# Hybrid encoder layer on one core: norm loads moved to ACT's queue, two additions and one product moved between engines, loads and gates reordered

## The chip, the cores and the metric

One core of a Trainium2 chip runs the whole layer. The metric is the device time of one launch in microseconds (us). Engines are called as in the profile: PE (matrix products), PEld (its weight loads), DVE, ACT and POOL (GpSimd), and SP, which here only issues transfers (DMAs). ACT and POOL issue DMAs too. Each engine works through its own list of instructions in order.

## What is computed

The input is 2048 positions of 1024 channels. One layer has three branches that share one input projection of the normalised input:

```
h = rms_norm(x, norm_g);  z = h @ w_in
ya = fourier_mix(za) * silu(za_gate)                       # branch A
yb = rwkv7_bidir(centred_shift(z_rwkv)) * silu(zb_gate)    # branch B
yc = mla(zq, zkv, zkr) * silu(zc_gate)                     # branch C, attention of 6 heads
merged = sum of sigmoid(z_merge[n]) * (y_n @ proj_n)
out = rms_norm(x + merged @ w_out, final_g)
```

Branch B is a recurrence with a 64x64 state for each of 6 heads, once forward and once backward in time; the two outputs y[0] + y[1] are summed and normalised head by head (mean, variance), and a bonus is added:

```
bonus = einsum('bthn,btdhn,hn->bth', r, k_dir, r_k);   y + bonus[..., None] * v
```

## The kernel before, in words

In order of time (the stretches are those of the profiled execution):

- Up to about 515 us: norm of x, first columns of the input projection, preparation of the attention.
- 515 to 930 us: `columns()` goes on with the projection on PE (L142 to L144 are the three products of one block). Between its blocks PE does the pieces of `units()`, the preparation of branch B: 24 windows (3 channel groups p of 128 channels x 8 stretches u of 256 positions), each for 2 directions d, so 48 sets. One set is: `unit_lora` loads the low-rank input `ul`; `unit_lowrank` (PE) makes `wps`; `unit_decay` turns it into `th`, `ia` (ACT, L656 to L659), the running sum `ls` (DVE, L662 for d=0, L664 for d=1), `ge` (ACT), `kd` or `kds`, and `BK` (half on DVE, half on POOL, L691 and L692); `unit_x` makes `X` (DVE and POOL, L701 and L702); `unit_gram` makes the small products and masks them (DVE, L718 and L720), and SP stores X.
- In the second set of a window, `unit_values` copies the transposed v to `vt` (ACT, L631) and SP stores it. One set later `unit_bonus` multiplies the bonus sum `bp` (PE, L731) by v into `bv` (L733), and SP stores `bv` (L734). `vt` and `bv` have the same tag "vt", with one buffer: `vt` of a window can be written only when `bv` of the window before has landed in memory. In ACT's list `vt` stands ahead of `th` of its set.
- 930 to 1475 us: the rest of the projection (merge gates z, then the attention's gates `gc`), the Fourier branch, and `inverses` (a chain of DVE operations, L758 and L760). Its last results are stored, and `recurrence` loads them: `seq_load` (L969 loads X, L971 loads W), first products `sps` (L984).
- 1475 to 1938 us: attention on PE (`scores`, `softmax`, `probs`, `values`) with the recurrence's 32 steps between its pieces. A unit is 128 queries of one head: four blocks `sc` of scores (L142 to L144), their eviction to S (DVE, L1307), exp (ACT, L1314), four transposes `tp` (PE, L1322) copied to `PT` (L1032 on DVE or L1033 on ACT, `ptd` says which).
- 1938 to 2262 us: attention with `rwkv_out` between its pieces: 8 blocks of 256 positions, each with loads (L1050: `ry0`, `ry1`, `rbv`, `rg`), the sum y + y1 (L1062), mean, variance, and the store. Then first weights of the output stage. From the end of the recurrence on, `self.merged` is true.
- 2262 to 2632 us: output stage.

What sets the order: the pieces of PE are placed by hand, and the background work is a generator (units, then inverses, then recurrence, then rwkv_out) that the columns or the attention advance by `step()`, two steps to an attention unit. A `yield` more or fewer in the generator so moves its PE work by a quarter of a unit. `wait2` is the number of empty steps ahead of the recurrence. The other engines' lists are made by a scheduler from what is emitted; the tile pools add the waits for free buffers.

Of the kernel before, what the change touches and what calls it, by code (L numbers as in the profile page):

```python
# [9 lines left out]
F32 = mybir.dt.float32  # L10
F32R = mybir.dt.float32r
I32 = mybir.dt.int32
AF = mybir.ActivationFunctionType
# [4 lines left out]
P = 128  # L18
# [72 lines left out]
class Trunk:  # L91
    def __init__(self, tc, ins, out, stop=99):
# [39 lines left out]
        self.wait2 = 12  # L132
# [226 lines left out]
    def columns(self):  # L359
# [8 lines left out]
        gates = [(O_ZCG + n * P, self.to_gate(self.gc_d[n], self.nc.gpsimd)) for n in range(3)]  # L368
        self.inproj(gates[0][0], P, gates[0][1])
        cols = [(self.weights(c0, P), consume) for c0, consume in gates[1:]]  # L370
        for tb in range(NTB):
            for w, consume in cols:
                self.project(w, P, tb, consume, True)
# [166 lines left out]
    def units(self):  # L540
        tc, nc = self.tc, self.nc
        with tc.tile_pool(name="un", bufs=1, side="right", reuse_waits="tile") as up, \
# [10 lines left out]
            ul = self.unit_lora(opened[0], 0, up)  # L553
# [4 lines left out]
            for s in range(2 * len(wins) + 2):  # L558
# [5 lines left out]
                if s < 2 * len(wins):  # L564
# [5 lines left out]
                    wps = self.unit_lowrank(w, d, ul, gps)  # L570
                    item = self.unit_decay(w, d, wps, up, ge)
# [3 lines left out]
                if s < 2 * len(wins):  # L575
# [4 lines left out]
                    if s + 1 < 2 * len(wins):  # L580
                        ul = self.unit_lora(opened[n + d], 1 - d, up)
# [56 lines left out]
    def unit_lora(self, w, d, up):  # L638
        lo = up.tile([P, 2, UN], F32R, tag="ul", name=f'ul{w["p"]}{w["u"]}{d}', bufs=self.ulb)
        self.nc.sync.dma_start(lo.bitcast(F32), self.lo_d[:, d, :, w["sl"]].rearrange("n p t -> p n t"))  # L640
        return lo
# [9 lines left out]
    def unit_decay(self, w, d, wps, up, ge):  # L651
# [27 lines left out]
        if d == 1:  # L679
            kds = w["kds"]  # L680
            nc.gpsimd.tensor_tensor(kds, kd, kds, ALU.add)
# [46 lines left out]
    def unit_bonus(self, w, up, gps):  # L728
# [4 lines left out]
        nc.vector.tensor_tensor(bv, bp[:, :UN], w["v"], ALU.mult)  # L733
# [200 lines left out]
    def recurrence(self):  # L934
        tc, nc = self.tc, self.nc
        with tc.tile_pool(name="sq", bufs=1, side="right", reuse_waits="tile") as sp, \
# [10 lines left out]
            yield  # L947
# [15 lines left out]
    def seq_load(self, sp, n):  # L963
# [3 lines left out]
        for d in range(2):  # L967
            c = n if d == 0 else NCH - 1 - n
            nc.sync.dma_start(X[:, d].rearrange("p n s t -> p n (s t)"), self.X_d[d][c])  # L969
            for h in range(2):  # L970
                nc.sync.dma_start(W[64 - 64 * h:P - 64 * h, d, :, 2 * h:2 * h + 2, :].rearrange("p n q k -> p n (q k)"),  # L971
                                  self.V_d[c * C:(c + 1) * C, :, h, :])
        return X, W
# [66 lines left out]
    def rwkv_out(self):  # L1040
        tc, nc = self.tc, self.nc
        W = 256
        with tc.tile_pool(name="ro", bufs=3, side="right", reuse_waits="tile") as rp, \
                tc.tile_pool(name="rops", bufs=1, space=PSUM, side="right", reuse_waits="tile") as rps:
            def load(b):
                sl = slice(b * W, (b + 1) * W)
                ts = []
                for n, src in (("ry0", self.y_d[0]), ("ry1", self.y_d[1]), ("rbv", self.bv_d), ("rg", self.gb_d)):
                    t = rp.tile([P, NP, W], F32, tag=n, name=f"{n}{b}")
                    nc.sync.dma_start(t, src[:, :, sl].rearrange("n p t -> p n t"))  # L1050
# [3 lines left out]
            nxt = load(0)  # L1054
            yield
            yield
            for b in range(T // W):
                sl = slice(b * W, (b + 1) * W)
                y, y1, bv, g = nxt
                if b + 1 < T // W:  # L1060
                    nxt = load(b + 1)
                nc.vector.tensor_tensor(y, y, y1, ALU.add)  # L1062
# [3 lines left out]
                yield  # L1066
                mu = rps.tile([P, 4, W], F32, tag="mu", name=f"mu{b}")
# [11 lines left out]
                self.blocksums(var, hi, lo)  # L1079
                va = rp.tile([P, NP, W], F32, tag="rva", name=f"rva{b}", bufs=1)  # L1080
# [235 lines left out]
    def probs(self, u, g):  # L1316
# [7 lines left out]
        self.copy(g in self.ptd, dst, tp)  # L1324

    def values(self, w):
# [4 lines left out]
        def piece(j):  # L1331
            for k in range(2 * j, 2 * j + 2):
# [3 lines left out]

# [160 lines left out]
```

## Time and profile before

| | |
|---|---|
| median of 3 runs | 2632.33 us (2628.31 to 2634.77) |
| profiled execution, its own time | 2634.32 us |
| its span | 2632.5 us |
| PE busy | 2504.7 us, 95% |
| DVE busy | 1737.4 us, 66% |
| ACT busy | 991.9 us, 38% |
| POOL busy | 848.0 us, 32% |
| mean granted clock of PE | 0.982 |

The busy shares are means over stages that differ, so the stages are read apart: which engine waits in each, and for whom. PE is the engine with the most work, and what the other engines cost shows as PE's idle time. The profiled execution is 2.0 us above the median.

### The profile page before, as it was taken

What the parts mean: (1) busy time and instruction counts of PE and PEld (TensorE: products, weight loads), DVE (VectorE), ACT (ScalarE), POOL (GpSimd) and SP (SyncE); (2) the same over time, 40 slices, a digit from 0 to 9 for tenths busy, and PEclk for the clock granted to TensorE, in tenths of its full rate; (3) what the DMA queues carried; (4) which work ended last, traced back from release to release, by engine and by line L of the source; (5) the groups of instructions that cost most, each with busy time, mean ns of one, the idle gap of its engine ahead of it and who ended that gap; (6) DMA issues with size and microseconds to landing.
All of it is one profiled execution on the core that took longest, in us unless ns stands there. A gap on an engine that the chain in (4) does not pass through costs nothing.

```text
span 2632.5 us, 46308 instructions
## 1 busy us (share of the span) xinstructions
PE 2504.7 (95%) x17295; PEld 2040.8 (78%) x17295; DVE 1737.4 (66%) x3432; ACT 991.9 (38%) x1929; POOL 848.0 (32%) x1124
## 2 busy tenths in 40 slices
PE   7989999999999999989998899999998899999998
PEld 6778887877777777768776688878876677799997
DVE  6236564388888859579398567766767787544444
ACT  6354443355555521111113333333355565322221
POOL 2244433355555511212220233323322220334342
PEclk9999999999999999999998899999999999999999
DMA  4353434477777774552733655665544311645452
GB/s 167 95 146 121 149 125 157 141 262 256 245 262 247 246 156 128 130 145 86 136 84 111 157 169 186 192 186 166 174 149 125 101 53 59 194 128 154 131 154 78
DMA packets 318443, 404.86 MB, mean 154 GB/s; under 512 B 56078, under 2 KB 225097, under 8 KB 317130
## 3 DMA queue, kind: packets, MB, share of 16 engines
q1 hardware_dynamic: 310762, 382.99, 49.0%
q0 software_dynamic: 7456, 18.91, 3.0%
q8 instruction: 137, 2.24, 0.4%
q14 instruction: 88, 0.72, 0.1%
HBM read 236.91 MB, written 164.89 MB: 153 GB/s over the span
## 4 chain that ended last, share of the span: by engine, by line
PE 38%; DVE 13%; DMA 8%; issue 4%; POOL 1%; ACT 1%; SPq 1%; DVEq 0%; POOLq 0%; ACTq 0%
PE av L1334 5%; PE tp L1322 4%; DVE M L760 4%; DVE tmp L758 4%; PE sc L142 3%; PE sc L144 2%; PE sc L143 2%; PE po L144 2%; PE po L143 2%; PE po L142 2%; PE p L144 2%; PE p L143 2%; PE p L142 2%; DVE S L1307 1%; PE mm L142 1%
## 5 line engine op out<-in xcount | busy, mean ns | idle before, releaser
L142 PE MATMUL mm<-hh,wh 128*128 128x512 f32 x1536 | 613.8, 400 | 6.5 <-ACT z L483 3.2
L144 PE MATMUL mm<-hh,wl 128*128 128x512 f32 x1536 | 604.0, 394 | 2.8 <-POOL wl L419 2.6
L143 PE MATMUL mm<-hl,wh 128*128 128x512 f32 x1536 | 605.2, 394 | 0.0
L142 PEld LDWEIGHTS mm<-hh,wh 128*128 128x128 f32 x1536 | 291.7, 190 | 72.1 <-ACT z L483 5.2
L144 PEld LDWEIGHTS mm<-hh,wl 128*128 128x128 f32 x1536 | 291.6, 190 | 65.1 <-POOL wl L419 4.1
L143 PEld LDWEIGHTS mm<-hl,wh 128*128 128x128 f32 x1536 | 291.9, 190 | 58.2 <-issue 1.0
L1307 DVE TENSOR_SCALAR_CACHE_REDUCE S<-sc 128x512 f32<-128x512 f32 x384 | 260.7, 688 | 73.2 <-PE sc L144 67.5
L419 POOL TENSOR_TENSOR wl<-wr,wh 128x256 fp32r<-128x256 f32 x192 | 172.2, 910 | 419.1 <-ACT wh L418 406.2
L1322 PEld LDWEIGHTS tp<-c_id,S 128*128 128x128 f32 x1536 | 192.9, 143 | 84.9 <-ACT PT L1033 14.5
L1322 PE MATMUL tp<-c_id,S 128*128 128x128 f32 x1536 | 237.8, 278 | 21.0 <-ACT S L1314 8.6
L1314 ACT ACTIVATE S<-S,m 128x2048 f32<-128x2048 f32 x96 | 192.2, 2003 | 161.7 <-DVE m L1312 161.7
L758 DVE TENSOR_TENSOR tmp<-M 128x62 f32<-128x62 f32 (+30 forms) x186 | 171.7, 923 | 96.5 <-DMA zm_d<-z 41.3
L142 PE MATMUL sc<-K,Q 96*128 96x512 f32 x384 | 188.4, 491 | 19.7 <-DVE S L1307 13.8
L1033 ACT ACTIVATE PT<-tp 128x512 f32<-128x512 f32 x192 | 113.2, 591 | 225.8 <-PE tp L1322 222.7
L1334 PE MATMUL av<-PT,V 128*64 128x256 f32 x1536 | 180.0, 385 | 0.0
L760 DVE TENSOR_TENSOR M<-M,tmp 128x62 f32<-128x62 f32 (+30 forms) x186 | 170.7, 918 | 5.8
L418 ACT ACTIVATE wh<-wr 128x256 fp32r<-128x256 f32 x192 | 74.4, 412 | 238.7 <-DMA wr<-in_w_in_dram 149.2
L144 PE MATMUL sc<-K,Q 96*128 96x512 f32 x384 | 155.4, 405 | 0.0
L143 PE MATMUL sc<-K,Q 96*128 96x512 f32 x384 | 154.8, 403 | 0.0
L483 ACT ACTIVATE z<-mm 128x512 f32<-128x512 f32 (+1 forms) x120 | 70.3, 589 | 217.7 <-PE mm L144 107.2
L1334 PEld LDWEIGHTS av<-PT,V 128*64 128x64 f32 x1536 | 105.4, 137 | 57.8 <-issue 11.2
L1432 POOL TENSOR_TENSOR g<-g 128x256 f32<-128x256 f32 x128 | 98.8, 774 | 143.2 <-DVE g L1430 100.6
(388 smaller groups left out, 4945.4 us busy)
## 6 DMA issues: line engine op xcount, KB each, us to landing
X_d<-X SPq DMA_DIRECT2D x96, 512.0 KB
sX<-X_d SPq DMA_DIRECT2D x64, 768.0 KB
wr<-in_w_in_dram SPq DMA_DIRECT2D x193, 128.0 KB
zm_d<-z SPq DMA_DIRECT2D x96, 256.0 KB
g<-zm_d SPq DMA_DIRECT2D x64, 384.0 KB
uu<-u_d SPq DMA_DIRECT2D x24, 512.0 KB
ul<-lo_d SPq DMA_DIRECT2D x48, 256.0 KB
sW<-V_d SPq DMA_DIRECT2D x128, 96.0 KB
```

The source lines that it names most:

```text
L142: mm(out, lh, rh, start=start, stop=False)
L143: mm(out, lh, rl, start=False, stop=False)
L144: mm(out, ll, rh, start=False, stop=stop)
L419: nc.gpsimd.tensor_tensor(wl[:, ks, :], wr, wh[:, ks, :].bitcast(F32), ALU.subtract)
L758: nc.vector.tensor_tensor(tv, M[:, 0:j, j:j + 1].to_broadcast([P, j, n]), M[:, j:j + 1, j + 1:C].to_broadcast([P, j, n]), ALU.mult)
L760: nc.vector.tensor_tensor(M[:, 0:j, j + 1:C], M[:, 0:j, j + 1:C], tv, ALU.add)
L1033: return self.nc.scalar.activation(out, src, AF.Copy)
L1307: nc.vector.tensor_scalar(u["S"][:, ks], sc, 1.0, -3.4e38, ALU.mult, ALU.max, accum_out=u["m4"][:, kb:kb + 1])
L1314: nc.scalar.activation(S, S, AF.Exp, scale=SM_SCALE, bias=m4[:, 5:6], accum_out=u["win"]["rs"][:, col:col + 1])
L1322: nc.tensor.transpose(tp[:, k, :], u["S"][:, (4 * g + k) * P:(4 * g + k + 1) * P], self.ident)
L1334: nc.tensor.matmul(av[64 * h:64 * h + 64, 0:QB], self.V[:, k, (2 * hp + h) * 64:(2 * hp + h + 1) * 64], PT[k // 4][:, k % 4, h, :], start= ...
L1432: nc.gpsimd.tensor_tensor(g, g, acc, ALU.add)
```

## The change

1. `wait2` goes from 12 to 9, and `recurrence` yields three times instead of once after its first loads: the first loads are emitted three steps earlier and the first products one step earlier, 9 + 3 steps instead of 12 + 1.
2. The gates `gc` are stored from ACT's queue instead of POOL's, and the last two gate columns are done in pairs of position blocks.
3. `unit_lora`'s load `ul` goes from SP's queue to ACT's, half a set earlier (48 loads).
4. The addition of `kds` for d=1 goes from POOL to DVE (24 times).
5. `unit_bonus`: one DVE product becomes a copy by ACT and a product on POOL (24 times).
6. `seq_load` loads W ahead of X.
7. `rwkv_out`: the four loads of a block go from SP's queue to ACT's, two blocks ahead instead of one; the sum y + y1 goes from DVE to POOL, one block ahead; a block has one step more.
8. `probs`: from `merged` on, one of the two copies on DVE goes to ACT.
9. `values`: doubling and inverting the row sums moves from ahead of the first piece into the fourth.

```diff
-        self.wait2 = 12
+        self.wait2 = 9
...
-        gates = [(O_ZCG + n * P, self.to_gate(self.gc_d[n], self.nc.gpsimd)) for n in range(3)]
+        gates = [(O_ZCG + n * P, self.to_gate(self.gc_d[n], self.nc.scalar)) for n in range(3)]
...
-        for tb in range(NTB):
+        for tbs in ((0, 1), (2, 3)):
             for w, consume in cols:
-                self.project(w, P, tb, consume, True)
+                for tb in tbs:
+                    self.project(w, P, tb, consume, True)
...
                     wps = self.unit_lowrank(w, d, ul, gps)
+                    if s + 1 < 2 * len(wins):
+                        ul = self.unit_lora(wins[n + d], 1 - d, up)
...
-                    if s + 1 < 2 * len(wins):
-                        ul = self.unit_lora(opened[n + d], 1 - d, up)
...
-        self.nc.sync.dma_start(lo.bitcast(F32), self.lo_d[:, d, :, w["sl"]].rearrange("n p t -> p n t"))
+        self.nc.scalar.dma_start(lo.bitcast(F32), self.lo_d[:, d, :, u * UN:(u + 1) * UN].rearrange("n p t -> p n t"))
...
-            nc.gpsimd.tensor_tensor(kds, kd, kds, ALU.add)
+            nc.vector.tensor_tensor(kds, kd, kds, ALU.add)
...
-        nc.vector.tensor_tensor(bv, bp[:, :UN], w["v"], ALU.mult)
+        nc.scalar.activation(bv, bp[:, :UN], AF.Copy)
+        nc.gpsimd.tensor_tensor(bv, bv, w["v"], ALU.mult)
...
-            yield
+            for _ in range(3):
+                yield
...
         for d in range(2):
             c = n if d == 0 else NCH - 1 - n
-            nc.sync.dma_start(X[:, d].rearrange("p n s t -> p n (s t)"), self.X_d[d][c])
             for h in range(2):
                 nc.sync.dma_start(W[64 - 64 * h:P - 64 * h, d, :, 2 * h:2 * h + 2, :].rearrange("p n q k -> p n (q k)"),
                                   self.V_d[c * C:(c + 1) * C, :, h, :])
+        for d in range(2):
+            c = n if d == 0 else NCH - 1 - n
+            nc.sync.dma_start(X[:, d].rearrange("p n s t -> p n (s t)"), self.X_d[d][c])
...
-                    nc.sync.dma_start(t, src[:, :, sl].rearrange("n p t -> p n t"))
+                    nc.scalar.dma_start(t, src[:, :, sl].rearrange("n p t -> p n t"))
...
-            nxt = load(0)
+            tiles = [load(0), load(1)]
...
-                nc.vector.tensor_tensor(y, y, y1, ALU.add)
+                if b == 0:
+                    nc.gpsimd.tensor_tensor(y, y, y1, ALU.add)
...
+                yield
+                if b + 2 < T // W:
+                    tiles.append(load(b + 2))
...
+                if b + 1 < T // W:
+                    nc.gpsimd.tensor_tensor(tiles[b + 1][0], tiles[b + 1][0], tiles[b + 1][1], ALU.add)
...
-        self.copy(g in self.ptd, dst, tp)
+        self.copy(g in (self.ptd[1:] if self.merged else self.ptd), dst, tp)
...
+            if j == 3:
+                nc.vector.tensor_scalar(rs, rs, 2.0, None, ALU.mult)
+                nc.vector.reciprocal(rs, rs)
...
-        nc.vector.tensor_scalar(rs, rs, 2.0, None, ALU.mult)
-        nc.vector.reciprocal(rs, rs)
```

How instructions move, at three places. In the names, the figures after the letters are p, u and d, so `bv12` is the bonus of p=1, u=2, and `BK130` is of p=1, u=3, d=0; the last number only tells tiles apart. The lines of the changed kernel are some lower or higher numbers than those of before for the same code (L692 is there L694).

POOL in the units, p=1, window u=3, direction d=0, before:

```order
404 L673 COPY gc_127<-ge0_4620 128x4
405 L701 TENSOR_TENSOR X130_6929<-uu13_6709,ge0_4620 64x4x64
406 L702 TENSOR_TENSOR X130_6929<-uu13_6709,ge0_4620 64x4x64
407 L691 TENSOR_TENSOR BK130_6865<-ia130_6852,th130_6850 64x4x64
408 L692 TENSOR_TENSOR BK130_6865<-kds13_6860,th130_6850 64x4x64
409 L419 TENSOR_TENSOR wl3488_7344<-wr3488_0_7345,wh3488_7343 128x256
```

and now, the same place:

```order
403 L675 COPY gc_127<-ge0_4620 128x4
404 L703 TENSOR_TENSOR X130_6940<-uu13_6721,ge0_4620 64x4x64
405 L704 TENSOR_TENSOR X130_6940<-uu13_6721,ge0_4620 64x4x64
406 L693 TENSOR_TENSOR BK130_6877<-ia130_6864,th130_6862 64x4x64
407 L694 TENSOR_TENSOR BK130_6877<-kds13_6872,th130_6862 64x4x64
408 L736 TENSOR_TENSOR bv12_6897<-bv12_6897,uu12_6523 128x256
409 L420 TENSOR_TENSOR wl3488_7359<-wr3488_0_7360,wh3488_7358 128x256
```

The bonus product of the window before comes to stand behind both X and both BK of d=0.

ACT at the end of the recurrence, before:

```order
1364 L1027 ACTIVATE ys0_31_18643<-sps1_12919 128x192
1365 L1027 ACTIVATE ys1_31_18646<-sps1_12919 128x3x64
1366 L1033 ACTIVATE PT150_18337<-tp15110_18659 128x4x128
1367 L1033 ACTIVATE PT152_18401<-tp15112_18697 128x4x128
1368 L1033 ACTIVATE PT160_18733<-tp16000_18734 128x4x128
1369 L1314 ACTIVATE S1601_18652,rs16_18329<-S1601_18652,m41601_18653 128x2048
1370 L807 ACTIVATE rhim0_18761<-ry00_18684 128x768
```

and now, from a little later (`ys` is the last output of the recurrence, `y_d` where it is stored):

```order
1450 L1324 ACTIVATE S1600_18597,rs16_18375<-S1600_18597,m41600_18598 128x2048
1451 L1056 DMA ry00_18681<-y_d0_74 128x3x256
1452 L1039 ACTIVATE PT151_18395<-tp15111_18718 128x4x128
1453 L1056 DMA ry10_18683<-y_d1_75 128x3x256
1454 L1039 ACTIVATE PT152_18442<-tp15112_18729 128x4x128
1455 L1056 DMA rbv0_18685<-bv_d_70 128x3x256
1456 L1056 DMA rg0_18687<-gb_d_63 128x3x256
1457 L1056 DMA ry01_18689<-y_d0_74 128x3x256
1458 L1324 ACTIVATE S1601_18700,rs16_18375<-S1601_18700,m41601_18701 128x2048
1459 L1056 DMA ry11_18691<-y_d1_75 128x3x256
1460 L1039 ACTIVATE PT160_18768<-tp16000_18769 128x4x128
1461 L1056 DMA rbv1_18693<-bv_d_70 128x3x256
```

The loads stand between the exps and the PT copies, and PT copies of g=1 (the figure behind the window in `PT151`) are in the list as well.

PE at the start of the recurrence, before:

```order
6080 L1322 MATMUL tp01102_12943<-c_id_115,S0110_12746 128x128 x4
6081 L142 MATMUL sc02003_12949<-K00_12471,Q02_12740 128x512
6082 L143 MATMUL sc02003_12949<-K00_12471,Q02_12740 128x512
6083 L144 MATMUL sc02003_12949<-K00_12471,Q02_12740 128x512
6084 L1322 MATMUL tp01103_12954<-c_id_115,S0110_12746 128x128 x4
6085 L984 MATMUL sps0_12918<-sW_0_12929,sX_0_12928 64x64 x12
```

and now:

```order
6073 L142 MATMUL sc02001_12951<-K00_12495,Q02_12762 128x512
6074 L143 MATMUL sc02001_12951<-K00_12495,Q02_12762 128x512
6075 L144 MATMUL sc02001_12951<-K00_12495,Q02_12762 128x512
6076 L1332 MATMUL tp01101_12956<-c_id_115,S0110_12768 128x128 x4
6077 L990 MATMUL sps0_12850<-sW_0_12861,sX_0_12860 64x64 x12
6078 L142 MATMUL sc02002_12976<-K00_12495,Q02_12762 128x512
```

Two blocks of scores with their transposes (`sc02002`, `sc02003`), half a unit, which stood ahead of the first product of the recurrence, now stand behind it.

## Rows read from the trace of the kernel before

**Rows 1.** Windows view: stretch, its us, busy us (instructions) of each engine, clock, DMA
```profile
500.00:900.00 400.00, 382.72 (x2322) 314.18 (x2321) 325.84 (x560) 210.18 (x492) 226.47 (x305) 0.99 0.76 251
1930.00:2270.00 340.00, 308.75 (x2136) 233.39 (x2135) 249.51 (x620) 189.74 (x261) 60.21 (x49) 0.97 0.34 98
```

**Rows 2.** Waits of PE, 490 to 950 us: total us, times, longest
```profile
PE bp L731 <- DVE kds L682: 12.3, 9, 2.0
PE wps L648 <- DMA ul<-lo_d: 6.2, 8, 1.6
```

**Rows 3.** Line L664, one execution per window: ns min/median/max, first and last start
```profile
L664 DVE TENSOR_TENSOR_SCAN ls<-c_rst,th x24: 691/692/1217, 519.9 to 912.7; 128x256 f32<-128x256 f32 x24
```

**Rows 4.** Timeline of one window: start us, us, instruction, idle before and its end
```profile
656.95 0.69 DVE L664 TENSOR_TENSOR_SCAN ls<-c_rst,th 128x256 f32<-128x256 f32 x1 [2.02 <-ACT th L659]
...
664.26 0.69 DVE L662 TENSOR_TENSOR_SCAN ls<-c_rst,th 128x256 f32<-128x256 f32 x1
...
666.36 0.41 DVE L733 TENSOR_TENSOR bv<-bp,uu 128x256 f32<-128x256 f32 x1
...
666.79 0.33 SPq L734 DMA_DIRECT2D bv_d<-bv  x1
...
668.64 0.74 POOL L692 TENSOR_TENSOR BK<-kds,th 64x256 f32<-64x256 f32 x1
...
669.94 0.60 ACT L631 ACTIVATE vt<-vp 128x512 f32<-128x512 f32 x1 [2.48 <-DMA bv_d<-bv]
...
673.37 0.46 ACT L656 ACTIVATE th<-wps,derived 128x256 f32<-128x256 f32 x1
...
674.62 0.69 DVE L664 TENSOR_TENSOR_SCAN ls<-c_rst,th 128x256 f32<-128x256 f32 x1 [3.92 <-ACT th L659]
```

**Rows 5.** Waits of ACT, 490 to 930 us
```profile
ACT vt L631 <- DMA bv_d<-bv: 49.5, 18, 4.1
...
ACT wh L418 <- DMA wr<-in_w_in_dram: 26.9, 18, 2.8
```

**Rows 6.** Groups of POOL, 490 to 930 us: busy, mean ns, idle before
```profile
L681 POOL TENSOR_TENSOR kds<-kd,kds 128x256 f32<-128x256 f32 x24 | 21.2, 884 | 47.6 <-DVE kd L678 44.6 <-issue 2.4
```

**Rows 7.** Waits of PE, 1300 to 1500 us
```profile
PE sps L984 <- DMA sW<-V_d: 10.2, 2, 7.4
PE sc L142 <- DVE zg L473: 5.8, 1, 5.8
```

**Rows 8.** Timeline around the first product of the recurrence
```profile
1460.66 1.45 SPq L969 DMA_DIRECT2D sX<-X_d  x1
...
1466.71 1.18 SPq L971 DMA_DIRECT2D sW<-V_d  x2
...
1471.57 0.84 PE L984 MATMUL sps<-sW,sX 128*64 128x64 f32 x4 [7.39 <-DMA sW<-V_d]
```

**Rows 9.** Timeline of PE: two score blocks that follow each other
```profile
1447.94 0.50 PE L142 MATMUL sc<-K,Q 96*128 96x512 f32 x1
...
1449.10 0.48 PE L142 MATMUL sc<-K,Q 96*128 96x512 f32 x1
```

**Rows 10.** Waits of PE, 1930 to 2270 us
```profile
PE sc L142 <- DVE S L1307: 13.8, 5, 6.5
PE tp L1322 <- ACT PT L1033: 6.7, 8, 2.8
PE tp L1322 <- ACT S L1314: 4.8, 2, 2.5
PE tp L1322 <- DVE PT L1032: 4.7, 9, 2.7
```

**Rows 11.** Groups of DVE, 1930 to 2270 us
```profile
L1032 DVE COPY PT<-tp 128x512 f32<-128x512 f32 x84 | 57.6, 686 | 13.6 <-PE av L1334 11.0 <-PE tp L1322 2.6
...
L1062 DVE TENSOR_TENSOR ry<-ry,ry 128x768 f32<-128x768 f32 x8 | 8.6, 1074 | 21.7 <-issue 11.2 <-DMA ry<-y_d 10.5
```

**Rows 12.** Groups of ACT, 1930 to 2270 us
```profile
L1033 ACT ACTIVATE PT<-tp 128x512 f32<-128x512 f32 x84 | 49.3, 589 | 66.7 <-PE tp L1322 63.6 <-PE av L1334 2.9
```

More of the change, by code (lines that the diff above doesn't have):

```diff
@@ L552, in units @@
                 self.lora_weights(0, d, up)
-            ul = self.unit_lora(opened[0], 0, up)
+            ul = self.unit_lora(wins[0], 0, up)
             self.rate = 2
@@ L638, in unit_lora @@
     def unit_lora(self, w, d, up):
-        lo = up.tile([P, 2, UN], F32R, tag="ul", name=f'ul{w["p"]}{w["u"]}{d}', bufs=self.ulb)
-        self.nc.sync.dma_start(lo.bitcast(F32), self.lo_d[:, d, :, w["sl"]].rearrange("n p t -> p n t"))
+        p, u = w
+        lo = up.tile([P, 2, UN], F32R, tag="ul", name=f"ul{p}{u}{d}", bufs=self.ulb)
+        self.nc.scalar.dma_start(lo.bitcast(F32), self.lo_d[:, d, :, u * UN:(u + 1) * UN].rearrange("n p t -> p n t"))
         return lo
@@ L1058, in rwkv_out @@
                 sl = slice(b * W, (b + 1) * W)
-                y, y1, bv, g = nxt
-                if b + 1 < T // W:
-                    nxt = load(b + 1)
-                nc.vector.tensor_tensor(y, y, y1, ALU.add)
+                y, y1, bv, g = tiles[b]
+                if b == 0:
+                    nc.gpsimd.tensor_tensor(y, y, y1, ALU.add)
                 hi, lo = [rp.tile([P, NP, W], F32R, tag=t, name=f"{t}m{b}", bufs=1) for t in ("rhi", "rlo")]
```

## The prediction

> **What bounds the kernel now.** I read the windows of the profile first, then what PE waits for in each stage, then the waits of the engine that it waits for. PE is at work for 382.72 of the 400 us from 500 to 900, and for 308.75 of the 340 us after the recurrence [rows 1]: 17 and 31 us are all that can be won there. In the first stage PE waits for the bonus sum's input and for `ul` [rows 2], 18.5 us. Both are ends of the same loop. Its 24 windows begin at 519.9 to 912.7, a pitch of 392.8/23 = 17.08 us [rows 3], and PE's own share of it is 0.957 x 17.08 = 16.3 us.
>
> The loop can be followed in one window [rows 4]. From `ls` of d=1 to `ls` of d=0: 7.31 us, in which DVE does not rest. From there to the end of `bv` on DVE (666.77): 2.51. Then `bv` is stored, and ACT's `vt`, which shares its buffer, starts at 669.94: 3.17 later, after an idle wait of 2.48 for that transfer. `th` starts 3.43 later, and the next `ls` 1.25 after that. The sum is 17.67, the window's pitch. Of the 3.43, `vt` itself holds ACT for some 0.5; the other 2.9 are a `wh` that stands between and waits for weights. Over all windows ACT waits 49.5 us for `bv`'s store and 26.9 us for weights [rows 5]. Without weights the loop takes 14.8 us, with them 17.7; windows of both kinds alternate.
>
> Before the recurrence PE waits 10.2 us for data that the inverses' last store releases, and 5.8 us for a gate [rows 7]. After it, PE waits 13.8 + 4.7 us for DVE, 4.8 for exp and 6.7 for ACT's PT copies [rows 10]. There DVE stands idle for 21.7 us ahead of `ry` + `ry1` [rows 11], whose loads come late, and PE's scores queue up behind it.
>
> **Units: +23 us.** Bonus, `kds` and `ul` act on one loop, so they go together. The bonus product no longer runs on DVE early in the set; it is the last of five POOL operations. POOL's BK before it ends at 669.38 [rows 4], 5.12 us after `ls` instead of the 2.51 at which `bv` was done. The product itself isn't in the trace; the nearest row is POOL's two-input operation of the same shape, 0.884 us [rows 6]. ACT's copy ahead of it is done meanwhile. Only then can SP store `bv`. The other terms stay: 7.31 + 5.12 + 0.88 + 3.17 + 0.5 + 1.25 = 18.23 us. The weight waits go, since the second pair of `wh` now stands behind `th` and hides in the longer wait for `bv`. So the alternation of 14.8 and 17.7 becomes an even 18.2: (18.23 - 17.08) x 23 = +26. In four windows `vt` now stands behind `th` and `ia`, which take it some 0.85 us off the loop: -3. That leaves +23.
>
> Bounds: PE alone allows no pitch under 16.3, (16.3 - 17.08) x 23 = -17. The longest wait for the store is 4.1 instead of 2.48 [rows 5], 1.6 us more a window: +60. I take the window's own 3.17, which is near the middle. The `kds` addition on DVE costs one operation like `bv`'s 0.41 [rows 4], and takes away a POOL operation that ran beside DVE; I count both as nothing, since at worst they add 0.4 x 23 = 9 us, inside the bounds. It removes the 12.3 us that PE waits for `kds`, and the earlier `ul` removes 6.2 [rows 2], but PE then waits for the loop instead. The 48 `ul` issues on ACT lie in its wait for `bv`'s store.
>
> POOL's 0.884 us stands against 0.41 for DVE's product [rows 4, 6]. The Trainium skill (GPSIMD Engine Reference, Engine selection) gives adds and products to VectorE and calls GpSimd about twice as slow for two inputs; the trace agrees, 884 to 410 ns. By that rule alone the move would cost 0.47 x 23 = 11 us; the place in POOL's queue, which the rule doesn't speak of, makes it 23.
>
> **Start of the recurrence: +4 us.** Two score blocks move behind the first product. A block takes 1449.10 - 1447.94 = 1.16 us [rows 9]; they filled PE while it waited, and now come after it: +2.3. X's first load was issued at 1460.66, ahead of the wait for V's halves; now all four W go first, at 0.59 us each from 1466.71 [rows 8], and X after them. The last of the six loads is issued at most 1.9 us later than the first product's data before: I take +1.5, and 0 to 8 for the whole.
>
> **Gates: -1 us.** PE's 5.8 us for the gate may go, but PE then arrives earlier at the same wait for the inverses, whose DVE chain sets the end [rows 7]. Only what frees that chain counts; bounds -4 and +1.
>
> **After the recurrence: -17 us.** From DVE go the sums (8.6 us), the idle time ahead of them (21.7), and half of the 84 PT copies, 42 x 0.686 = 29 us [rows 11]: 59 of 340 us. So PE's waits for DVE, 13.8 + 4.7, go [rows 10], and half of those for exp, 2.4, since exp waits for DVE's maxima. ACT takes 42 x 0.589 = 25 us of copies [rows 12] and 32 issues. What an issue costs ACT isn't shown; SP's are 0.59 [rows 8], together 19 us. ACT's busy time goes from 189.7 to 234 of some 323 us. I let PE's 6.7 us for ACT's copies grow by 4: 18.5 + 2.4 - 4 = 17. Bounds: nearly all of the 30 listed goes, with some lost clock (0.97 mean [rows 1]): -28; ACT's waits double and the first `ry1` load, which waits for the recurrence's last store, holds ACT for 4 us: -8. The sums on POOL, about twice their 1.07 us, run a block ahead, hidden by POOL's idle time: 60 of 340 us busy [rows 1]; without that cover the eight cost 17 us, the rows' 8.6 doubled. The row sums' inversion only moves behind three value pieces on PE, which hide it; if they didn't, PE would wait two small DVE operations in each window of attention.
>
> **Sum.** 2634.3 + 23 + 4 - 1 - 17 = 2643.3 for the profiled execution, which is 2.0 above the median: 2641. A measurement of this kernel can tell about 0.3%, 7.9 us, from no change: faster is below 2624.4, slower above 2640.2.
>
> **The rivals.**
> - *The store is short, so the loop isn't longer* (faster; chance 0.24). `bv` is now issued 3.5 us later, when the X stores ahead of it are more nearly done. If the 3.17 falls to 2.3, the loop takes 17.36, the units cost +3 instead of +23, and the time is 2621; if PE becomes the bound, -17 and 2601. It decides where the leg from product to `vt` is under 2.0 us (no loss) to 2.7 (half of it). For it: the wait ranges widely. Against: even the quiet window that I show has 3.17. The Trainium skill (DMA: Bandwidth & Descriptors, Anatomy of one DMA) gives about 2.0 us fixed plus the bytes at 436 GB/s, for GpSimd's path, 2.3 us for this store as an estimate; the trace's 3.15 from issue to `vt` differs, so the measurement decides.
> - *ACT becomes the bound after the recurrence, and the store leg is longer* (slower still; 0.17). Then that stage gives 8 instead of 17, 2650; with a leg of 4 us, 19 us more, 2669. For it: loads in ACT's list hold its copies while they wait. Against: ACT is busy for 70% only.
> - *The last stage gives all it can* (0.14). -28 instead of -17 with the loop as forecast: 2630, no change that can be told.
> - *The loads aren't earlier after all* belongs to the second: ACT's list has them behind exps, and the first waits for the same store as before. It alone would make 8 of the 17.
>
> **How the numbers follow.** The forecast has 0.45, with 2633 to 2650 as its own range. Faster gets most of the first rival, 0.24. No change gets the third rival and 0.4 of the forecast's range, 0.33. Slower gets the rest, 0.43. The range reaches from the middle of the first rival, 2613, to the second, 2657.
>
> **What would show it.** Right: the start of `ls` (d=1) has a pitch near 18.2; ACT's wait for `bv`'s store grows from 49.5 to some 100 us or more, its wait for weights falls; PE's idle time from 500 to 930 grows by 20 or so, named after `th`, `X` or BK. The first `sps` runs behind `tp01101` with its wait longer. After the recurrence PE's waits for DVE's S are near 0, and those for ACT's PT near 10. Wrong: a pitch of 17.1 or less, with the product early on POOL or a store leg near 2 us; or ACT's idle time after the recurrence gone and PE's waits there above 22 us.

## The result, and the profile after

The changed kernel takes 2670.86 us (median of 4 runs, 2659.56 to 2673.32), the kernel before beside it 2633.55: ratio 1.0137, 95% interval 1.0105 to 1.0169. It is slower by 37 us, where the prediction had 2641 and a range up to 2657. The profiled execution took 2673.32 us, its span is 2671.5, 39.0 us longer than before's. The sign was right, the size was not.

Three lines by their first and last start tell where the 39 us arise. Before: first products of the recurrence, its last, and the last row of values of the attention.

```profile
L984 PE MATMUL sps<-sW,sX x768: 219/222/369, 1471.6 to 1924.3; 128*64 128x64 f32 x192
L1022 PE MATMUL sps<-sX,uz x768: 222/222/222, 1492.2 to 1935.8; 128*64 128x64 f32 x192
L1348 DVE TENSOR_TENSOR yc<-av,gt x24: 418/424/425, 1457.6 to 2264.0; 128x256 f32<-128x256 f32 x24
```

After: the same three, and ahead of them the `ls` of d=1, which answers to [rows 3].

```profile
L666 DVE TENSOR_TENSOR_SCAN ls<-c_rst,th x24: 691/692/693, 523.4 to 949.3; 128x256 f32<-128x256 f32 x24
L990 PE MATMUL sps<-sW,sX x768: 219/222/369, 1506.9 to 1969.4; 128*64 128x64 f32 x192
L1028 PE MATMUL sps<-sX,uz x768: 222/222/314, 1522.0 to 1982.6; 128*64 128x64 f32 x192
L1358 DVE TENSOR_TENSOR yc<-av,gt x24: 394/425/426, 1492.8 to 2305.0; 128x256 f32<-128x256 f32 x24
```

| stretch | before | after | difference | predicted |
|---|---|---|---|---|
| to the first `ls` (d=1) | 519.9 | 523.4 | +3.5 | 0 |
| 23 windows of the units | 392.8 | 425.9 | +33.1 | +23 |
| to the first product of the recurrence | 558.9 | 557.6 | -1.3 | +3 |
| recurrence | 464.2 | 475.7 | +11.5 | 0 |
| to the last row of values | 328.2 | 322.4 | -5.8 | -17 |
| to the end of the span | 368.5 | 366.5 | -2.0 | 0 |

The windows view, which answers to [rows 1], shows the same: in the units PE works 373 us of 400 instead of 383, at a mean granted clock of 0.95. After the recurrence the stage is taken from the last product to the last row of values, first before, then after: PE works 297 to 298 us in both, and its idle time falls from 31 to 25 us.

```profile
500.00:900.00 400.00, 373.48 (x2139) 302.22 (x2137) 315.68 (x512) 197.41 (x471) 201.21 (x279) 0.95 0.69 229
...
1935.80:2264.00 328.20, 297.56 (x2025) 223.42 (x2020) 239.99 (x594) 184.19 (x253) 57.31 (x44) 0.97 0.33 95
...
1982.60:2305.00 322.40, 296.94 (x2038) 223.34 (x2034) 213.93 (x553) 204.74 (x297) 71.96 (x52) 0.98 0.34 98
```

PE's waits in the units (490 to 970 us) answer to [rows 2]. The wait for `kds` is halved, the one for `ul` has grown from 6.2 to 9.9 us, though its load was moved ahead, and the small products wait for DVE's X.

```profile
PE g L717 <- DVE X L722: 10.9, 15, 0.8
PE wps L650 <- DMA ul<-lo_d: 9.9, 3, 3.9
PE bp L733 <- DVE kds L684: 5.5, 6, 1.5
```

The waits of ACT in the units (490 to 970 us, total, times, longest) answer to [rows 5]. The wait for the bonus's store has grown from 49.5 to 94.8 us, that for weights has fallen from 26.9 to 6.9, and there is a new one: `th` waits for DVE's BK.

```profile
ACT vt L632 <- DMA bv_d<-bv: 94.8, 22, 5.6
ACT th L658 <- DVE BK L693: 62.4, 22, 3.4
...
ACT wh L419 <- DMA wr<-in_w_in_dram: 6.9, 12, 1.6
```

One window of the loop, in the timeline (start, us, instruction), to be laid beside [rows 4]. DVE first:

```profile
674.41 0.69 DVE L666 TENSOR_TENSOR_SCAN ls<-c_rst,th 128x256 f32<-128x256 f32 x1 [2.98 <-ACT th L661]
675.02 0.40 DVE L680 TENSOR_TENSOR kd<-kd,uu 128x256 f32<-128x256 f32 x1
675.52 0.42 DVE L683 TENSOR_TENSOR kds<-kd,kds 128x256 f32<-128x256 f32 x1
675.86 0.42 DVE L687 TENSOR_TENSOR ia<-ia,uu 128x256 f32<-128x256 f32 x1
676.20 0.91 DVE L703 TENSOR_TENSOR X<-uu,ge 64x256 f32<-64x256 f32 x1
677.03 0.91 DVE L704 TENSOR_TENSOR X<-uu,ge 64x256 f32<-64x256 f32 x1
677.87 0.96 DVE L684 SCALAR_TENSOR_TENSOR kds<-uu,vec,kds 128x256 f32<-128x256 f32 x1
678.75 0.95 DVE L694 TENSOR_TENSOR BK<-kd,th 64x256 f32<-64x256 f32 x1
679.63 0.41 DVE L693 TENSOR_TENSOR BK<-ia,th 64x256 f32<-64x256 f32 x1
...
682.58 0.67 DVE L664 TENSOR_TENSOR_SCAN ls<-c_rst,th 128x256 f32<-128x256 f32 x1
...
692.34 0.69 DVE L666 TENSOR_TENSOR_SCAN ls<-c_rst,th 128x256 f32<-128x256 f32 x1 [3.50 <-ACT th L661]
```

Then POOL, SP and ACT, each from its own timeline of the same window:

```profile
676.08 0.75 POOL L703 TENSOR_TENSOR X<-uu,ge 64x256 f32<-64x256 f32 x1
...
686.80 0.74 POOL L694 TENSOR_TENSOR BK<-kds,th 64x256 f32<-64x256 f32 x1
687.62 0.74 POOL L736 TENSOR_TENSOR bv<-bv,uu 128x256 f32<-128x256 f32 x1
```

```profile
682.72 0.87 SPq L727 DMA_DIRECT2D X_d<-X  x2
...
688.38 0.33 SPq L737 DMA_DIRECT2D bv_d<-bv  x1
```

The first line of SP is the pair of X stores ahead of the bonus's store. Before, in the window of [rows 4], they stand here:

```profile
664.42 0.87 SPq L725 DMA_DIRECT2D X_d<-X  x2
```

ACT:

```profile
690.59 0.60 ACT L632 ACTIVATE vt<-vp 128x512 f32<-128x512 f32 x1 [4.72 <-DMA bv_d<-bv]
691.08 0.47 ACT L658 ACTIVATE th<-wps,derived 128x256 f32<-128x256 f32 x1
```

The prediction's loop can be read off: 682.58 - 674.41 = 8.17 (it had 7.31); from there to the product's end, 687.62 + 0.74 - 682.58 = 5.78 (5.12 + 0.88 = 6.00); to `vt` 2.23 (3.17); to `th` 0.49; to `ls` 1.26. Together 17.93. This window is one of the short ones: the mean pitch is 425.9/23 = 18.52, and in every window over 18.2 DVE's stretch takes 8.7 to 9.9 us. The means over the 23 windows are 8.78 for DVE's stretch, 5.68 to the product's end, 2.40 for the store's leg and 1.66 from `vt` to the next `ls`. So the product's place was nearly as forecast, the store's leg is 0.8 shorter, and DVE's stretch 1.5 longer than the 7.31. Most of this 1.5 isn't the change's: before, the same stretch takes 7.30 to 9.91 us, 8.20 on average, and the 7.31 comes from one of the shortest windows.

PE's waits in the recurrence (1500 to 1990 us): before, it waited 1.3 us for sX there.

```profile
PE sps L990 <- DMA sX<-X_d: 21.9, 7, 9.8
```

9.8 and 1.6 of it belong to the start, where PE waited 10.2 us for W before [rows 7]; some 10.5 are spread over the stage.

```profile
1506.86 0.57 PE L990 MATMUL sps<-sW,sX 128*64 128x64 f32 x4 [9.80 <-DMA sX<-X_d]
```

PE's waits after the recurrence (1960 to 2310) answer to [rows 10]:

```profile
PE tp L1332 <- ACT PT L1039: 17.1, 23, 2.1
PE var L177 <- POOL rlov L811: 4.8, 1, 4.8
PE mu L177 <- POOL rlom L811: 1.5, 1, 1.5
PE tp L1332 <- ACT S L1324: 1.2, 1, 1.2
```

DVE's S is gone from the list, as forecast, and ACT's PT has grown by 10 instead of 4 us. The 6.3 us for POOL's `rlov` and `rlom`, parts of the norm of y, are new.

### The profile page after: what moved, and what is told of

Read it like the earlier page. It is cut to its first block, busy times and chain, and to the rows that moved or that the text cites. A ratio compares the mean times of both kernels' runs of the same rounds, so it can differ in the third digit from the quotient of the medians.

```text
span 2671.5 us, 46203 instructions
## 1 busy us (share of the span) xinstructions
PE 2523.0 (94%) x17295; PEld 2051.8 (77%) x17295; DVE 1730.7 (65%) x3383; ACT 1017.8 (38%) x1994; POOL 852.3 (32%) x1120
## 5 line engine op out<-in xcount | busy, mean ns | idle before, releaser
L1332 PE MATMUL tp<-c_id,S 128*128 128x128 f32 x1536 | 235.7, 276 | 23.5 <-ACT PT L1039 17.1
L1039 ACT ACTIVATE PT<-tp 128x512 f32<-128x512 f32 x233 | 135.7, 591 | 211.3 <-PE tp L1332 201.3
```

The lines of the kernel that those rows point to most:

```text
L1039: return self.nc.scalar.activation(out, src, AF.Copy)
L1332: nc.tensor.transpose(tp[:, k, :], u["S"][:, (4 * g + k) * P:(4 * g + k + 1) * P], self.ident)
```

## The experiments

Each is told with its median beside the median of the kernel before from the same chip; this lies at 2630.4 to 2633.6 us on all of them, so two runs from different chips can be compared to about 3 us. Stretches within a kernel are read from one profile of each run. How far they scatter can be read where the code is the same: nine runs whose units are those of r7 take 379.4 to 381.1 us for the 23 windows. Two theories stood against each other in the units: **A**, the product on POOL holds the store and the shared buffer; **B**, the addition on DVE makes DVE's stretch longer.

**r1: the bonus alone undone in the changed kernel.**

```diff
-        nc.scalar.activation(bv, bp[:, :UN], AF.Copy)
-        nc.gpsimd.tensor_tensor(bv, bv, w["v"], ALU.mult)
+        nc.vector.tensor_tensor(bv, bp[:, :UN], w["v"], ALU.mult)
```

> The changed kernel with the bonus product alone back on DVE. Theory A (the product's place as the last of five POOL operations makes the loop of the 24 windows long): the loop loses 5.68 - 2.4 = 3.3 us, so the pitch falls from 18.5 to PE's own 16.3 to 17.1 and the time by 33 to 45 us, to about 2626 to 2638. Theory B (the kds addition on DVE, which lengthens the stretch from ls d=1 to ls d=0 from 8.2 to 8.8 us, makes it long): the pitch stays near 18 and the time falls by 10 us at most, to about 2660.

2657.53 us (before 2632.43; ratio 1.0112, 1.0088 to 1.0135). Its windows have a pitch of (932.2 - 518.7)/23 = 17.98, 12.4 us less than the changed kernel's. The pitch is theory B's (near 18), and the time falls by 13 us, a little more than its 10.

```profile
L666 DVE TENSOR_TENSOR_SCAN ls<-c_rst,th x24: 673/692/1192, 518.7 to 932.2; 128x256 f32<-128x256 f32 x24
```

**r2: the kds addition alone undone in the changed kernel** (`nc.vector` back to `nc.gpsimd` in that line).

> The changed kernel with the kds addition alone back on POOL. Theory A: the stretch from ls d=1 to ls d=0 loses 0.4 to 0.8 us, the pitch falls by as much, the time by 9 to 18 us, to about 2653 to 2662. Theory B: the pitch falls to 17.1 or less and the time by 33 us or more, to 2638 or less.

2648.42 us (1.0069, 1.0042 to 1.0096). Pitch (928.9 - 517.5)/23 = 17.89, 14.5 us less: within theory A's 9 to 18 for the addition, and short of B's 33, so each of the two edits accounts for a part. The median falls by 22, which is more than A had; in the profile 6 of it lie ahead of the first window.

```profile
L666 DVE TENSOR_TENSOR_SCAN ls<-c_rst,th x24: 691/692/693, 517.5 to 928.9; 128x256 f32<-128x256 f32 x24
```

**r3: X ahead of W again in the changed kernel** (the loop of `seq_load` as before).

> The changed kernel with X loaded ahead of W again in the recurrence. Theory C (X stands behind W loads that wait for a buffer, so it lands late all through the recurrence): PE's waits for sX after the first step fall from 12 us to about 1, the recurrence from 476 to 466 us, the time by 9 to 12 us. Rival D (the stage is longer because it starts half a unit earlier): waits and time stay within 3 us.

2668.52 us (1.0149, 1.0121 to 1.0177), the same as the changed kernel within its spread. In its one profile the recurrence took 468 us instead of 476 and PE waited less for sX, which would speak for theory C; the median doesn't show it, and n1 and n2 below speak against it.

**r6: the shared buffer alone taken away in the changed kernel.** `kds` has been read by the bonus sum when `bv` is written, so its tile can hold `bv`.

```diff
-        bv = up.tile([P, UN], F32, tag="vt", name=f"bv{p}{u}")
+        bv = w["kds"]
```

> The changed kernel with bv written into the tile of kds, which has been read by then, instead of the buffer that it shares with vt; the product stays on POOL. Theory E (the product on POOL costs time only through the shared buffer: vt waits for the store of bv): ACT's wait of 95 us for bv's store goes, the pitch falls to 16.3 to 17.1, the time by 33 to 45 us, to 2626 to 2638. Rival F (POOL's longer queue itself holds X and BK): the pitch stays above 18, the time within 10 us of 2671.

2633.09 us (1.0007, 0.9989 to 1.0024). ACT's wait for the bonus's store is gone, and the units take 388.9 us, 3.9 less than before, with the product still on POOL and the addition still on DVE. The last `ls` starts at 909.3, and PE works 385.81 us of 400 at a granted clock of 1.00:

```profile
L666 DVE TENSOR_TENSOR_SCAN ls<-c_rst,th x24: 673/673/1024, 520.4 to 909.3; 128x256 f32<-128x256 f32 x24
```

```profile
500.00:900.00 400.00, 385.81 (x2324) 316.11 (x2323) 348.62 (x560) 215.90 (x514) 229.01 (x306) 1.00 0.75 248
```

So most of what the moved operations cost, they cost because they lie on a loop that the shared buffer closes. Not all of it: r7 below has the same tile without the moves, and its units take 379.9 us. With the shared buffer the moves cost 33.1 us, without it 388.9 - 379.9 = 9.0; r12 (388.6) and eight more runs with r7's units bear this out. In r6 DVE is nearly the bound of the loop: it waits 3.8 us in total ahead of the 24 `ls` (d=1), and 33.1 us in r7.

**r8: bonus, addition and the order of X and W undone in the changed kernel; the `ul` loads stay on ACT's queue.**

> The changed kernel with three edits undone: bonus product and kds addition where they were, X ahead of W. Theory A+B (the product on POOL and the addition on DVE each make some 17 to 19 us of the units' 36): the last ls (d=1) is back at 913 to 918 us instead of 950, the time at 2620 to 2632. Rival G (the ul loads on ACT's queue cost as well): it stays 10 us or more behind 913, the time at 2640.

2643.23 us (1.0032, 1.0017 to 1.0047). The last `ls` is where theory A+B had it; the time isn't, it is 3 us over rival G's. The pitch is (916.3 - 519.9)/23 = 17.23, 3.6 us more than before over the 23 windows: the `ul` loads cost a little. Two pairs of runs that differ in the units by `ul` alone agree: there r1 takes 4.7 us more than n3, and r2 3.9 more than r5 (n3 and r5 are below). In the profile the recurrence is 9.6 us longer than before's and the stage after it 6.2 shorter; that execution (span 2635.4) was faster than the median, so the rest of the 10 us can't be placed.

```profile
L666 DVE TENSOR_TENSOR_SCAN ls<-c_rst,th x24: 673/692/1245, 519.9 to 916.3; 128x256 f32<-128x256 f32 x24
```

**r5: the bonus alone put into the kernel before** (r1's diff the other way).

> The kernel before with the bonus as a copy by ACT and a product on POOL, nothing else. By the prediction's own sum for the loop with the store's leg at 2.4 us, as the changed kernel has it: 7.3 to 8.2 + 5.0 + 0.75 + 2.4 + 0.5 + 1.3 = 17.3 to 18.2 us of pitch, 5 to 25 us more than before, 2638 to 2657. Rival H (the weight loads behind wh keep their own wait): pitch 18.5 or more, over 2660.

2644.72 us (1.0043, 1.0026 to 1.0060). Pitch (924.8 - 517.3)/23 = 17.72, +14.7 us over the windows, +11.2 in the median.

```profile
L664 DVE TENSOR_TENSOR_SCAN ls<-c_rst,th x24: 690/692/693, 517.3 to 924.8; 128x256 f32<-128x256 f32 x24
```

**n3: the addition alone put into the kernel before.**

```diff
-            nc.gpsimd.tensor_tensor(kds, kd, kds, ALU.add)
+            nc.vector.tensor_tensor(kds, kd, kds, ALU.add)
```

> The kernel before with the kds addition alone on DVE. Theory B' (one more DVE operation in the loop, and one more of its neighbours slowed by POOL): the stretch from ls d=1 to ls d=0 grows by 0.8 us, pitch 17.7 to 17.9, time 2645 to 2652. The prediction's count: 0 to 9 us, 2632 to 2641.

2642.53 us (1.0035, 1.0022 to 1.0047). Pitch (926.5 - 517.8)/23 = 17.77, +15.9 us over the windows: the pitch is as theory B' had it; the time, 10.5 us more than before, lies between its range and the prediction's. The two edits alone and what r8 keeps make 14.7 + 15.9 + 3.6 = 34.2 us beside the 33.1 of all: in the windows they add up.

```profile
L664 DVE TENSOR_TENSOR_SCAN ls<-c_rst,th x24: 691/692/1093, 517.8 to 926.5; 128x256 f32<-128x256 f32 x24
```

The terms of the loop, as means over the 23 windows of each run's profile, in us:

| | `ls` (d=1) to `ls` (d=0) | to the bonus product's end | to `vt` (store's leg) | to the next `ls` (d=1) | pitch |
|---|---|---|---|---|---|
| predicted | 7.31 | 6.00 | 3.17 | 1.75 | 18.23 |
| before | 8.20 | 2.43 | 3.40 | 3.04 | 17.08 |
| changed kernel | 8.78 | 5.68 | 2.40 | 1.66 | 18.52 |
| r1: addition on DVE, `ul` | 8.63 | 1.66 | 4.31 | 3.38 | 17.98 |
| r2: product on POOL, `ul` | 7.89 | 5.80 | 2.43 | 1.77 | 17.89 |
| r5: product on POOL | 7.66 | 5.80 | 2.60 | 1.65 | 17.72 |
| n3: addition on DVE | 8.88 | 2.37 | 3.56 | 2.95 | 17.77 |

Before against r5 and n3 against the changed kernel, a product that ends 3.3 us later shortens the next two terms by more than 2 together: the store's leg is shorter, and most of the wait for weights goes. The addition on DVE, before against n3 and r2 against the changed kernel, lengthens the first term alone, by 0.68 and 0.89.

**r7: the shared buffer taken away in the kernel before** (r6's diff).

> The kernel before with bv in the tile of kds instead of the buffer that it shares with vt, nothing else. Theory E (the shared buffer holds the loop of before as well): ACT's 49.5 us of waiting for the store go, the pitch falls from 17.08 toward PE's 16.3, the time by up to 17 us, to 2616 to 2626. Rival I (weights, ul and kds take the wait's place): within 4 us of 2632.

2618.03 us (0.9944, 0.9924 to 0.9963): one line makes the kernel before 15 us faster. The pitch is (896.9 - 517.0)/23 = 16.52, near PE's 16.3.

```profile
L664 DVE TENSOR_TENSOR_SCAN ls<-c_rst,th x24: 673/692/1273, 517.0 to 896.9; 128x256 f32<-128x256 f32 x24
```

**r12: r6 and r3 together.**

> The changed kernel with bv in the tile of kds and X ahead of W. Theories C and E: the units' 36 us and the recurrence's 8 to 12 us both go, what is left is the change's gain after the recurrence, 3 to 6 us: 2620 to 2628. Rival: the gain after the recurrence is nil and the time is that of before, 2632.

2634.59 us (1.0012, 0.9997 to 1.0027), a miss: the rival held. PE's wait for sX in the recurrence was 6.4 us, though X stood first. The last row of values comes 1.6 us earlier than before's, the last product of the recurrence 3.9 us later: the units' loss is gone, but the recurrence still takes 471.6 us, 7.4 more than before, and only some 5 are gained after it.

The next four start from r7 and try the edits after the recurrence. The stage runs from the last product of the recurrence to the last row of values; on r7 it takes 2247.2 - 1919.6 = 327.6 us.

**m1: the change's `rwkv_out` and `values` on r7; both PT copies stay on DVE.**

> The kernel before with bv in the tile of kds (2618 us), plus the change's norm stage (loads on ACT's queue two blocks ahead, sums on POOL, one step more) and the row sums' inversion in the fourth piece; both PT copies stay on DVE. Theory J (after the recurrence ACT is the bound of the changed kernel, through the PT copies that it was given): from the last step of the recurrence to the last value row the stage falls from 328 us by more than the changed kernel's 6, to 310 to 318, and the time to 2604 to 2612; PE waits 7 us or less for ACT's PT. Theory K (DVE needs the relief of the copies): PE's waits for DVE come back, 10 us or more, and the stage stays at 322 or more.

2603.27 us (0.9884, 0.9867 to 0.9902); the stage 2231.0 - 1921.0 = 310.0. PE's waits from 1920 to 2250:

```profile
PE tp L1326 <- ACT PT L1033: 12.2, 8, 3.7
```

The gain is as theory J had it, its 7 us of waiting for ACT are 12.2. PE's wait for POOL's `rlov` isn't there, though the loads are on ACT's queue.

**m2: m1 with the 32 loads on SP's queue.**

```diff
-                    nc.scalar.dma_start(t, src[:, :, sl].rearrange("n p t -> p n t"))
+                    nc.sync.dma_start(t, src[:, :, sl].rearrange("n p t -> p n t"))
```

> The run before this with the 32 loads on SP's queue, still two blocks ahead. If loads in ACT's list hold ACT (theory L): 2 to 6 us faster than with ACT's queue, PE's wait for POOL's low half of the split, 6 us in the changed kernel, gone. If the queue does not matter: within 2 us in that stage.

2594.55 us (0.9853, 0.9832 to 0.9874); the stage 2225.2 - 1922.8 = 302.4. PE's waits from 1920 to 2250:

```profile
PE tp L1326 <- ACT PT L1033: 7.6, 8, 1.9
```

The issues in ACT's list cost 7.6 us in the stage (8.7 by the medians), more than theory L's 2 to 6. So the queue didn't help. What did is among the other edits there, the loads two blocks ahead, the sums on POOL, the step more and the row sums' inversion, which weren't tried apart.

**m3: m1 with the PT copies of g = 1 on ACT.**

> The same base with all of the change's edits after the recurrence, the PT copies on ACT too. Theory J: the stage at 322 to 325 us as in the changed kernel, 4 to 12 us longer than with the copies on DVE, PE waiting 13 us or more for ACT's PT; time 2611 to 2616. Theory K: the stage under 315.

2609.28 us (0.9907, 0.9878 to 0.9935); the stage 2239.8 - 1920.8 = 319.0, 9 us more than m1 (6 by the medians). PE waits for ACT 22 times:

```profile
PE tp L1326 <- ACT PT L1033: 20.1, 22, 2.7
```

**m4: r7 with the PT copies on ACT and the row sums' inversion moved, the norm stage as before.**

> The same base with the PT copies of g = 1 on ACT and the row sums' inversion moved, the norm stage as before. Theory J: DVE's idle time ahead of its sums (21.7 us) stays, and PE waits for DVE's S as well as for ACT's PT: stage 324 to 330 us, time within 4 us of 2618. Theory K: stage under 318.

2616.38 us (0.9932, 0.9914 to 0.9949); the stage 2248.8 - 1923.0 = 325.8. The wait for DVE's S stays and the one for ACT is added:

```profile
PE tp L1322 <- ACT PT L1033: 14.9, 18, 2.1
PE sc L142 <- DVE S L1307: 10.9, 5, 4.6
```

**n1: m2 with W ahead of X** (the change's `seq_load`).

> The best kernel so far (bv in the tile of kds, norm stage of the change with loads on SP's queue, PT copies on DVE; 2594.6 us) with W loaded ahead of X. Theory C (order of the loads): from the first product of the recurrence to its last 466.8 us becomes 472 to 478, PE waits 8 us or more for sX, the time 2600 to 2606. Theory D (the earlier start): within 2 us.

2592.44 us (0.9848, 0.9833 to 0.9863). The recurrence takes 1920.3 - 1457.2 = 463.1 us, m2's 466.7. Theory C falls: the order alone costs nothing.

**n2: m2 with the recurrence's earlier start.**

```diff
-        self.wait2 = 12
+        self.wait2 = 9
...
-            yield
+            for _ in range(3):
+                yield
```

> The same base with the start of the recurrence half a unit earlier (9 steps and 3 instead of 12 and 1), loads in the old order. Theory D: PE waits 5 us or more for sX in the recurrence, which takes 470 us or more, the time 2598 to 2604. Theory C: within 2 us of the base in that stage.

2607.31 us (0.9901, 0.9886 to 0.9916), 13 us more than m2 and 3 more than theory D had. The generator is advanced twice in an attention unit, so a `yield` moves its work by half a unit, not by the quarter named ahead. The recurrence takes 1925.3 - 1450.6 = 474.7 us instead of m2's 1922.8 - 1456.1 = 466.7, and PE's waits from 1445 to 1930 have 8.3 us for sX, with X first:

```profile
PE sps L985 <- DMA sW<-V_d: 12.2, 2, 9.6
PE sps L985 <- DMA sX<-X_d: 8.3, 5, 2.5
```

So theory D holds, and all runs agree. The eight kernels with the earlier start (the changed one, r1, r2, r3, r6, r8, r12, n2) take 467.7 to 475.7 us for the recurrence, the eleven without it 462.8 to 466.6; the means are 472.0 and 464.8. Among the eight the order shows nothing: with W first 468.6 to 475.7, with X first 467.7 to 474.7.

The earlier start costs time after the recurrence too: n2's stage takes 308.9 us, m2's 302.4. PE's wait for `rlov` and `rlom` is in all eight, 4.8 us in n2 and 5.5 to 6.5 in the others, and in the six kernels that have the change's norm stage without the earlier start it is 0.5 us at most.

**n4: m2 with the gates' edits.**

> The best kernel so far with the gates gc stored from ACT's queue and the last two gate columns in pairs. The prediction's term: -1 us (-4 to +1), since the inverses' chain on DVE sets the end: 2591 to 2596. Rival: PE's wait for the gate goes and the chain is helped, -5 us or more.

2590.38 us (0.9830, 0.9811 to 0.9849), 4 us less than m2 by the medians, with ranges that overlap (2581.8 to 2593.1 and 2591.2 to 2599.7).

**n5: n4 and n1 together.**

> The kernel with bv in the tile of kds, the change's norm stage with loads on SP's queue, the gates' edits, and W ahead of X. If the gates' 4 us and the order's 0 to 2 us are independent: 2586 to 2590. If they meet at the same wait for the inverses: 2590 to 2594.

2587.56 us (0.9838, 0.9814 to 0.9862), the fastest here: 43 us less than the kernel before beside it, 83 less than the changed one.

## Why the prediction was right and wrong

- *Units, the loop*: right in kind, too small in size: +23 predicted, 33.1 measured. The loop was closed by the buffer that `vt` and `bv` share, and the product's place as POOL's last of five is on it: r6 takes the buffer away and 24 of the 33 us with it. The step that failed is "The other terms stay: 7.31". This is DVE's stretch of one window that happens to be among the shortest; it is 8.20 on average before and 8.78 after. So the term was 1.5 us too small in each window, 34 us in all. The store's leg, 3.17, was 0.8 too large (18 us), and the product's place 0.3 too large (7 us), so the forecast of the pitch, 18.23, came near 18.52 in part by luck. Nor do windows of 14.8 and 17.7 us alternate: the 13 windows of before in which `th` directly follows `vt` take 15.2 to 17.9.
- *Units, the `kds` addition*: this step failed. The prediction counted it "as nothing, since at worst they add 0.4 x 23 = 9 us"; alone it makes 15.9 us in the windows and 10.5 in the time (n3). Nearly all of it is DVE's stretch, 8.88 instead of 8.20 on average, against 0.42 us for the operation. The window shows how: DVE's stretch holds four operations of 0.91 to 0.96 us where the one before held three, so 0.34 for the place of the new operation and 0.5 for one slowed neighbour. The POOL operation that left let POOL begin its X sooner, at 676.08, beside both of DVE's X. That this alignment is the cause is read from the two windows; it wasn't tried apart.
- *Units, `ul`*: counted as hidden, it makes 3.6 us in the windows (r8). PE's wait for it was to go and has grown to 9.9 us. Another 3.5 stand ahead of the first window, where the prediction had nothing; the other kernels with the same code up to there begin their first window at 517.5 to 521.0, so this isn't clear of scatter.
- *Start of the recurrence, +4*: the sum was near, the mechanism half right. The earlier start makes the recurrence 7 us longer on average, 11.5 in the changed kernel, and 2.3 of it are the two score blocks, which now stand inside the stage, as forecast. The first product comes no sooner for it (557 and 556 us behind the last `ls`, on average over the eight and the eleven kernels), since PE waits longer for its data there. The step that failed is that the half unit was priced only at the first product: X's loads land late inside the stage, and the norm's `rlov` holds PE for some 5 us after it. W ahead of X, which was priced at +1.5, costs nothing (n1). Why a shift by half a unit delays X in some steps, and `rlov` later, stays open; r3, with the early start and X first like n2 and r12, waited less for X (2.8 us) than they.
- *Gates, -1*: -4 by n4's median, the end of the bounds; the runs don't tell it from -1.
- *After the recurrence, -17*: DVE's waits went, as forecast, and by more than forecast: with the copies left on DVE and the loads on SP's queue the stage falls by 25.2 us (m2). The step that failed is "PE's 6.7 us for ACT's copies grow by 4": they grew to 17.1. In the stage the loads in ACT's list cost 7.6 us (m1 against m2) and the copies on ACT 9 (m3 against m1), 16.6 together. That would leave 8.6; with the wait for `rlov` and `rlom`, which the forecast didn't have either, the changed kernel kept 5.8. ACT was busy for 205 of 322 us only, so its mean share was a poor guide: a copy that stands behind an exp of 2.0 us or a block of load issues comes late for PE, however idle ACT is on average. That is read from ACT's list; it wasn't tried apart.
- *The rivals*: the second ("ACT becomes the bound after the recurrence, and the store leg is longer") had 2650 to 2669 and named half of what happened: the stage gave 6 instead of its 8, while the leg was shorter, not longer. The first had the leg right (2.40 against its 2.3) and its outcome wrong, since DVE's stretch took back what the leg gave.

## What to carry to other kernels

When an operation moves between two engines in a loop, price its neighbours too: here an operation of 0.42 us made each window 0.69 us longer. Take the terms of a loop as means over all its windows; one window that happened to be short cost this forecast 0.9 us a window. Before costs are moved around on a loop, look for what closes it; here one tile shared by two stores did, and giving one of them another place was worth 15 us, as much as the norm stage with its loads on ACT's queue (m1). A change of nine edits should be taken apart: the norm stage was worth up to 25 us and was hidden by a moved copy, a moved queue, an earlier start and a longer loop.

## What the runs showed of the hardware

- The same store landed 0.9 us sooner when it was issued later in its set: 2.21 us from issue to `vt` in the window shown of the changed kernel (688.38 to 690.59) against 3.15 before [rows 4]. The means over the windows go the same way in every run: 4.26 us in r1, where it is issued 1.1 us after the last X store ahead of it, 3.38 before (1.9), 3.49 in n3 (1.9), 2.52 in r5 (5.0), 2.40 in r2 (5.2) and 2.37 in the changed kernel (5.2). That the X stores slow it is the likely reading; it wasn't tried with all else equal.
- DVE's operations on two inputs took 0.41 us or 0.91 us in the same window, and which of them took 0.91 changed with POOL's start. Of the 192 products of 64x256 on DVE in the units, 83 took some 0.9 us before and 143 in the changed kernel. Every one of these ran beside two-input operations of POOL for 0.66 us or more; the changed kernel's 49 products of 0.41 us did so for 0.12 us on average. It isn't the whole rule: of before's 86 products of 0.41 us, 16 had POOL at work beside them nearly throughout. An operation's mean duration hides this.
- The granted clock differed between kernels with the same work: a mean of 0.95 from 500 to 900 us in the changed kernel (PE busy 373 us, a tenth of the time at 1.2 instead of 2.4 GHz), 0.99 before and 1.00 in r6. For the same 23 windows (before, changed kernel, n3) PE is busy 376, 398 and 380 us, so 21 of the 33 us stand in its busy time and 12 in its idle time. n3 lost 16 us at a clock of 0.99, so the loop can be longer without the clock; and with PE idle for 29 us it kept its clock, so PE's waiting alone doesn't explain the fall. How much of the 33 us is clock wasn't separated.

```profile
519.90:912.70 392.80, 376.32 (x2305) 308.98 (x2304) 328.75 (x566) 208.32 (x488) 226.03 (x304) 0.99 0.75 251
...
523.40:949.30 425.90, 397.59 (x2307) 321.59 (x2308) 349.26 (x566) 213.33 (x510) 219.06 (x303) 0.95 0.69 231
...
517.80:926.50 408.70, 379.64 (x2310) 309.38 (x2308) 340.30 (x589) 207.01 (x488) 208.19 (x281) 0.99 0.72 241
```
